# A one-layer hybrid encoder kernel: the last query turns regrouped, four output-weight loads and splits moved to later slots

## The chip, the cores and the metric

The kernel runs on one core of a Trainium2 chip. The metric is the device time of one execution in microseconds (us), and the median over runs is what counts. Three runs of the kernel before gave 1401.51, 1400.05 and 1415.82 us. One further execution was recorded by the hardware profiler, and all views quoted here come from it. Its engines are called PE (TensorE, matrix products; PEld is its load of weights into the array), DVE (VectorE), ACT (ScalarE), POOL (GpSimd) and SP (SyncE, which here only issues transfers). "SPq", "ACTq" and "POOLq" are the queues of those engines.

## The reference: what is computed

The input is a sequence `x` of 2048 tokens with 1024 channels, laid out as a grid of 32 rows and 64 columns. One layer is applied:

```python
shift, scale, gate = split(silu(c) @ w_ada + b_ada, 3)
h = rmsnorm(x, norm_w) * (1 + scale) + shift
na_q, na_k, na_v, na_z, ml_q, ml_k, ml_v, ml_o, ml_z, gates = split(h @ w_in + b_in)
na_out = neighbourhood_attention(na_q, na_k, na_v, rpb) * silu(na_z)   # 8 heads of 64, window 8 x 16 on the grid
ml_out = norm(mlstm_forward + mlstm_backward, sigmoid(ml_o)) * silu(ml_z)   # 4 heads of 128
y = concatenate([na_out, ml_out]) @ w_out
return rmsnorm(x + gate * y, final_norm_w)
```

All of it is float32. The change touches how `na_q` (the attention queries, 512 of the columns of `h @ w_in`) is computed at the very end of the input projection, and when the rows of `w_out` are brought in.

## The kernel before, in words

A float32 product is made of three TensorE products of rounded parts (type fp32r). Each operand is split into a high part and a low part: `whi` and `wlo` for weights, `hhi` and `hlo` for activations. The splitting costs one ACT instruction (the high part, a copy) and one subtraction on POOL or DVE (the low part) per block.

**Token groups and weight columns.** The 2048 tokens form four groups of 512, numbered 0 to 3; group g holds the grid rows 8g to 8g+7. The weight columns of the last part of the input projection form 16 slices `s` of 128 columns: `s` 0 to 3 are the mLSTM gate path, 4 to 7 the attention gate path, 8 to 11 the attention keys, 12 to 15 the attention queries. One slice for one group is 24 matrix products of 128 x 512 (8 blocks of the 1024 input channels, three products for each), here called one group-turn. There are 64 of them, 1536 products.

**Turns.** `nq_gen` (L840 to L911) is a Python generator that emits these products one at a time. Its list `turns` says in which order the slices come and which groups each takes; for instance `(12, (1, 0))` is slice 12 for group 1 and then for group 0. Here turn i is the i-th entry of that list. A turn works on weights that lie in one half of a two-place buffer (`whi_a`, `wlo_a`; the half is i modulo 2). A turn needs a new load of weights unless the turn two places before it had the same slice. One load is: a transfer of 512 KB into the single buffer `rawq` (`nq_load`, L826), then the split (`nq_split`: ACT L834 or, for queries, L837; then POOL L835 or, for queries, DVE L838). Both are emitted in the first group of the turn before, after its seventh product, where the split of turn i+1 is followed at once by the load for the turn after it. Since `rawq` has one buffer, a load can start only when the split before it has read the buffer.

**Eviction and stores.** After 24 products ACT (L898) writes the high part of the query result to one of two buffers, which alternate, DVE (L899) writes the low part, and two transfers on ACT's queue store them to a scratch tensor `d_qna` in device memory (L864, 256 KB each, emitted after the seventh product of the next group-turn; L911 for the last). The eviction two group-turns later writes the same buffer again and so has to wait until these stores are done.

**The way into phase 2.** `pump(n)` takes n products from the generator; earlier stages (the mLSTM passes, `ml_pass2`) use it to fill PE. Phase 2 then does the attention in 16 patches of 8 x 16 queries with four units (pairs of heads) each: 64 units. `slot(n)` issues, in an order written out by hand, the scores of unit n (`stage_s`: PE L1336/L1337, DVE L1342, ACT L1343), the product with the values of unit n-2 (`stage_o`: PE L1379, DVE L1381), the transposes of unit n-1 (`stage_t`: PE L1364, ACT L1366), loads, the normalisation of unit n (`stage_n`, DVE), whatever the table `first` has for this slot, and at last `pump(22)` (12 from slot 5 on). Slots begin when 108 or fewer of the 1536 products are left; slot 4 pumps all that remain. From slot 5 on the pump takes products of the output projection (`outproj`, L1416): first weights 4 to 7 for both halves of the 1024 output columns, 12 products for each half, then weights 0 to 3.

**Output weights.** `w_out` has 8 blocks of 512 KB, already multiplied by the gate and kept in device memory as `d_wo`. They have no space of their own: blocks 0 to 3 are loaded over the low part of group 0's activations and split into the place of its high part; blocks 4 to 7 take the place of group 1. `load_w` (L1311) uses POOL's queue for blocks 0 to 3 and SP's for 4 to 7. Blocks 0 to 3 are loaded by the last turn itself (`lastload`), as its products leave the space; blocks 4 to 7 by the table `first`. `split_w` (L1316: ACT L1317, then DVE L1318) makes high and low parts. Before it can use blocks 4 to 7, group 1 must have had its last query turn.

**Order on an engine.** Each engine executes its instructions in the order given; a wait holds all that comes behind it on that engine or queue. Inside the slots the order is the one written out; before them a planner places instructions by priority. ACT, for example, has in slot 5: the conversion of the mLSTM half of the first patch (`mix_high`, L1389, first use of the output projection), the exponentials of unit 5, the conversion of the attention half (L1389 again), the copies of unit 4's transposes, and the rest.

Of the kernel before, what the change touches and what calls it, by code (L numbers as in the profile page):

```python
# [15 lines left out]
P = 128  # L16
# [38 lines left out]
def patch_ps(ap):  # L55
    return ap.rearrange("p (a r k) -> p a r k", a=4, k=16)


class Kernel:
# [762 lines left out]
    def nq_load(self, i, s):  # L822

        nc = self.nc
        raw = self.raw.tile([P, 4, 256], F32, tag="raw0", name=f"rawq_{i}").rearrange("p a b -> p (a b)").rearrange("p (k c) -> p k c", k=KT)
        (nc.gpsimd if i >= 27 else nc.sync).dma_start(raw, self.w_main[10 + s // 2, :, :, (s % 2) * P : (s % 2 + 1) * P])  # L826
        return i, s, raw

    def nq_split(self, i, s, raw):
# [10 lines left out]
    def nq_gen(self):  # L840
        nc = self.nc
        whi, wlo = self.wslot[0]
        both, upper, lower = range(NG), (3, 2), (1, 0)
        turns = [(s, both) for s in (0, 1, 2, 3)] + [(s, upper) for s in (4, 5, 6, 7, 8, 9, 10, 11, 12, 14, 13, 15)]
        turns += [(s, lower) for s in (8, 9, 10, 11, 4, 5, 6, 7)]
        turns += [(15, (1,)), (13, (1,)), (14, (1,)), (12, (1, 0)), (14, (0,)), (13, (0,)), (15, (0,))]
        order = [(i, s, g) for i, (s, gs) in enumerate(turns) for g in gs]
        needs = [i for i, (s, gs) in enumerate(turns) if i == 1 or i > 1 and s != turns[i - 2][0]]
        raw = self.nq_load(needs[0], turns[needs[0]][0])
        late, parity = [], False  # L850
        for i, s, g in order:
            off = (i % 2) * P
            kind, ct = ("mz", "nz", "k", "q")[s // 4], s % 4
            patch = kind != "k"
            col = {"mz": 20, "nz": 8, "k": 4, "q": 0}[kind] + ct
            bias = self.bcol[:, col : col + 1]
            ps = self.pp.tile([P, GT], F32, tag="pp", name=f"pq_{s}_{g}")
            for k in range(KT):
                w1, w2 = whi[:, k, off : off + P], wlo[:, k, off : off + P]
                for n, (w, h) in enumerate(((w1, self.hhi), (w1, self.hlo), (w2, self.hhi))):  # L860
                    nc.tensor.matmul(patch_ps(ps) if patch else ps, w, self.htok(h, g, k, patch), start=(k == 0 and n == 0), stop=(k == KT - 1 and n == 2))  # L861
                    if k == 2 and n == 0:
                        while late:
                            nc.scalar.dma_start(*late.pop(0))  # L864
                    if i == len(turns) - 1 and k % 2 and n == 2:
                        self.lastload(k // 2)
                    if k == 2 and n == 0:
                        if needs and needs[0] == i + 1:
                            needs.pop(0)
                            self.nq_split(*raw)  # L870
                            if needs:
                                raw = self.nq_load(needs[0], turns[needs[0]][0])
                    if k < KT - 1 or n < 2:
                        yield
            if kind == "k" and g in lower:

                for j in range(2):
                    rows, other = slice(j * HD, (j + 1) * HD), slice((1 - j) * HD, (2 - j) * HD)
                    cols = slice(j * T + g * GT, j * T + (g + 1) * GT)
                    hv = self.kk[ct][rows, cols]  # L880
                    nc.scalar.activation(hv, ps[rows], AF.Identity, bias=bias[rows])
                    nc.vector.scalar_tensor_tensor(self.kk[ct][other, cols], ps[rows], bias[rows], hv.bitcast(F32), ALU.add, ALU.subtract)
                yield
                continue
            parity = not parity
            if parity:
                both = self.qst.tile([P, 1032], F32R, tag="st", name=f"qst_{s}_{g}")
            else:
                both = self.raw.tile([P, 1024], F32R, tag="raw1", name=f"qst_{s}_{g}")
            hv, lv = both[:, 0:512], both[:, 512:1024]  # L890
            if kind in ("mz", "nz"):
                hv = hv.bitcast(F32)
                nc.scalar.activation(hv, ps, AF.Silu, bias=bias)
                dst = (self.d_zna if kind == "nz" else self.d_zml)[4 * g : 4 * g + 4, :, ct].rearrange("a p q -> p a q")
                nc.scalar.dma_start(dst, hv.rearrange("p (a q) -> p a q", a=4))
                self.zdone.add((kind, ct, g))
            else:
                nc.scalar.activation(hv, ps, AF.Identity, bias=bias)  # L898
                nc.vector.scalar_tensor_tensor(lv, ps, bias, hv.bitcast(F32), ALU.add, ALU.subtract)  # L899
                for e, part in enumerate((hv, lv)):  # L900
                    src = part.bitcast(F32).rearrange("p (a q) -> p a q", a=4)
                    if kind == "q":
                        dst = self.d_qna[e, ct // 2, 4 * g : 4 * g + 4, :, ct % 2].rearrange("a p q -> p a q")
                    else:
                        dst = self.d_kna[e, ct * P : (ct + 1) * P, g * GT : (g + 1) * GT].rearrange("p (a q) -> p a q", a=4)
                    late.append((dst, src))
            if (s, g) in ((15, 3), (15, 2)):
                self.freed.append(g)
            yield
        while late:  # L910
            nc.scalar.dma_start(*late.pop(0))  # L911
# [287 lines left out]
    def phase2(self):  # L1199
        nc = self.nc  # L1200
# [13 lines left out]
        b0, last_b = patches[0], patches[-1]  # L1214
# [66 lines left out]
        def load_z(b):  # L1281
            nc.gpsimd.dma_start(zs[pos[b] % 2], self.d_zna[b])
# [5 lines left out]
        def load_m(b):  # L1288
            nc.gpsimd.dma_start(mix_parts(b)[1][:, 4:, :].bitcast(F32), self.d_mix[b])

        def load_x(b):
            pr, pc = divmod(b, 4)
            x = flat(self.raw.tile([P, 4, 256], F32, tag=f"raw{pos[b] % 2}", name=f"xr_{b}"))
            nc.gpsimd.dma_start(x, xg[8 * pr : 8 * pr + 8, 16 * pc : 16 * pc + 16, :])
            L[b]["x"] = x
# [15 lines left out]
        def load_w(k):  # L1311
            (nc.gpsimd if k < 4 else nc.sync).dma_start(wolo[k].bitcast(F32), self.d_wo[k])
# [3 lines left out]
        def split_w(k):  # L1316
            nc.scalar.activation(wohi[k], wolo[k].bitcast(F32), AF.Copy)  # L1317
            nc.vector.tensor_tensor(wolo[k], wolo[k].bitcast(F32), wohi[k].bitcast(F32), ALU.subtract)  # L1318
# [148 lines left out]
        for t in pbuf:  # L1467
            nc.vector.memset(t, 0.0)
        b1 = patches[1]

        first = {
            0: [lambda: nc.sync.dma_start(zs[1], self.d_mix[b0])],
            1: [lambda: load_w(4), lambda: load_w(5)],
            2: [lambda: load_w(6), lambda: load_w(7)],
            3: [lambda: split_w(4), lambda: split_w(5)],
            4: [lambda: split_w(6), lambda: split_w(7), lambda: load_x(b0)],
            5: [lambda: load_z(b1)],
            6: [lambda: load_m(b1), lambda: split_w(0), lambda: split_w(1), lambda: load_x(b1)],
            7: [lambda: split_w(2), lambda: split_w(3)],
            8: [load_fnw],  # L1480
# [147 lines left out]
```

## Time and profile before

| quantity | value |
|---|---|
| runs | 1401.51, 1400.05, 1415.82 us; median 1401.51 |
| profiled execution | 1398.06 us, its span from first to last instruction 1396.2 us |
| mean granted TensorE clock | 0.987 |
| PE busy | 1310.7 us, 8052 products |
| DVE, ACT, POOL busy | 834.0, 529.7, 294.5 us |
| transfers | 264.72 MB, mean 190 GB/s |

The profiled execution is 3.45 us shorter than the median. Times inside it are counted from its first instruction. In a timeline row the first number is the start, the second the duration, then engine, line, operation, output and inputs; in brackets stands how long the engine had been idle before, and what released it. A row of waits gives the total, the number and the longest in us. A row of windows gives the stretch, its length, busy time and count of each engine, the granted clock (1.00 is full), the busy share of the 16 transfer engines (1 or a little over means that they are all busy) and GB/s. A group row gives the shortest, middle and longest duration in ns.

### The profile page before, as it was taken

Reading aid. Unit: us, or ns where it says so; the run is one execution under the profiler, and the core shown is the slowest. Engines: PE = TensorE matmul, PEld = TensorE weight load, DVE = VectorE, ACT = ScalarE, POOL = GpSimd, SP = SyncE. Lnnn points to the kernel's source line nnn. Section 1 sums busy time; section 2 is a strip of 40 time slices with the busy share of each in tenths; the row PEclk is TensorE's granted clock in tenths of the full one; section 3 lists DMA queues with packets and bytes.
Section 4 is the critical chain, followed back from the end, with each engine's and each line's share of the span. In section 5 each row is a group of like instructions: output and inputs, shape, how many; then the busy total and the mean of one; then the engine's idle time right before and its main releaser. Section 6 shows DMA issues by size and latency. Waiting matters only on the chain. (4 is left out here: it accounts for less than half of the span.)

```text
span 1396.2 us, 23375 instructions
## 1 busy us (share of the span) xinstructions
PE 1310.7 (94%) x8052; PEld 1124.3 (81%) x8052; DVE 834.0 (60%) x2565; ACT 529.7 (38%) x1131; POOL 294.5 (21%) x324
## 2 busy tenths in 40 slices
PE   2989999998999999999999998899998999999996
PEld 2989998898887787888888886788776888888885
DVE  6683423211355669067758876877536777777674
ACT  4642344532222323113323223323345555555551
POOL 4353221433101110002212011112412211111111
PEclk9999999999999999999999999999999999999999
DMA  9798548778367675455766868745779896876862
GB/s 315 230 301 206 122 124 222 203 189 208 109 129 210 141 194 163 144 167 159 212 189 216 251 204 232 211 131 168 203 210 253 184 233 158 196 197 170 192 161 75
DMA packets 269100, 264.72 MB, mean 190 GB/s; under 512 B 33499, under 2 KB 229083, under 8 KB 268983
## 3 DMA queue, kind: packets, MB, share of 16 engines
q1 hardware_dynamic: 177022, 185.92, 49.4%
q0 software_dynamic: 21936, 39.30, 11.5%
q10 hardware_dynamic: 70024, 38.02, 9.6%
q8 instruction: 64, 1.05, 0.3%
q14 instruction: 54, 0.43, 0.1%
HBM read 178.62 MB, written 92.72 MB: 194 GB/s over the span
## 5 line engine op out<-in xcount | busy, mean ns | idle before, releaser
L861 PE MATMUL pq<-hhi,whi_a 128*128 128x512 f32 x512 | 211.6, 413 | 5.6 <-ACT whi_a L837 4.8
L861 PE MATMUL pq<-hhi,wlo_a 128*128 128x512 f32 x512 | 211.7, 414 | 0.5 <-DVE wlo_a L838 0.5
L861 PE MATMUL pq<-hlo,whi_a 128*128 128x512 f32 x512 | 211.4, 413 | 0.0
L861 PEld LDWEIGHTS pq<-hhi,whi_a 128*128 128x128 f32 x512 | 98.4, 192 | 24.6 <-ACT whi_a L837 5.6
L1343 ACT ACTIVATE pbuf<-pbuf,mn 128x480 f32<-128x480 f32 (+5 forms) x128 | 76.3, 597 | 104.4 <-DVE mn L1342 104.4
L861 PEld LDWEIGHTS pq<-hhi,wlo_a 128*128 128x128 f32 x512 | 98.3, 192 | 19.1 <-DVE wlo_a L838 1.0
L861 PEld LDWEIGHTS pq<-hlo,whi_a 128*128 128x128 f32 x512 | 98.1, 192 | 18.1
L1416 PE MATMUL y<-hhi,whi_a 128*128 128x512 f32 x256 | 85.9, 405 | 3.7 <-ACT whi_a L1389 3.7
L1416 PE MATMUL y<-hhi,wlo_a 128*128 128x512 f32 x256 | 84.3, 399 | 0.0
L835 POOL TENSOR_TENSOR wlo_a<-rawq,whi_a 128x1024 fp32r<-128x1024 f32 x20 | 48.0, 2398 | 166.1 <-ACT whi_a L834 91.9
L1111 POOL TENSOR_TENSOR hm<-hm,ck 128x128 f32<-128x128 f32 x64 | 26.3, 412 | 265.2 <-DVE hm L1110 179.9
L425 PE MATMUL pvo<-whi_b,hhi 128*128 128x256 f32 x256 | 74.0, 289 | 6.9 <-DVE stvo L495 6.9
L1342 DVE CUSTOM_DVE_ANT_0 pbuf<-pS,tab 128x480 f32<-128x480 f32 (+5 forms) x128 | 64.8, 540 | 26.0 <-PE pS L1337 18.4
L1019 DVE TENSOR_SCALAR wv<-kv,gtile 128x129 f32<-128x129 f32 x120 | 38.7, 328 | 63.0 <-PE dc L1035 34.8
L1092 ACT ACTIVATE num<-px,gtile 128x129 f32<-128x129 f32 x120 | 38.2, 364 | 98.4 <-PE px L1087 76.9
L426 PE MATMUL pvo<-wlo_b,hhi 128*128 128x256 f32 x256 | 72.8, 284 | 0.0
L427 PE MATMUL pvo<-whi_b,hlo 128*128 128x256 f32 x256 | 72.8, 284 | 0.0
L495 DVE TENSOR_TENSOR stvo<-pvo,brow 128x256 f32<-128x256 f32 x64 | 26.5, 420 | 72.7 <-PE pvo L427 56.6
L710 ACT ACTIVATE dec<-dec,gtile 128x128 f32<-128x128 f32 x128 | 42.0, 392 | 68.9 <-POOL dec L706 52.4
L460 DVE TENSOR_TENSOR stv<-pv,brow 128x256 f32<-128x256 f32 x32 | 12.9, 422 | 84.9 <-PE pv L427 37.5
L1379 PE MATMUL pO<-pt,v 128*64 128x128 f32 (+3 forms) x832 | 60.5, 280 | 0.5 <-ACT pt L1366 0.5
L1364 PE MATMUL pT<-ident,pbuf 128*128 128x128 f32 (+2 forms) x416 | 59.1, 280 | 0.0
(299 smaller groups left out, 3578.8 us busy)
## 6 DMA issues: line engine op xcount, KB each, us to landing
ck<-d_ck SPq DMA_DIRECT2D x64, 384.5 KB
kv<-d_ck SPq DMA_DIRECT2D x120, 128.5 KB
rawq<-in_w_main_dram SPq DMA_DIRECT2D x27, 512.0 KB
raw<-in_w_main_dram SPq DMA_DIRECT2D x20, 512.0 KB
d_ck<-stvo SPq DMA_DIRECT2D x16, 514.0 KB
x<-in_x_dram SPq DMA_DIRECT2D x16, 512.0 KB
wada<-in_w_ada_dram SPq DMA_DIRECT2D x32, 256.0 KB
dec<-d_mneg SPq DMA_DIRECT2D x32, 256.0 KB
```

The lines of the kernel that those rows point to most:

```text
L425: nc.tensor.matmul(ps, lhi(k), rhi(k), start=(k == 0), stop=False)
L426: nc.tensor.matmul(ps, lhi(k), rlo(k), start=False, stop=False)
L427: nc.tensor.matmul(ps, llo(k), rhi(k), start=False, stop=(k == KT - 1))
L710: nc.scalar.activation(t[:, d, o, :], t[:, d, o, :], AF.Exp, bias=self.cols["g"][:, d, h, c : c + 1])
L835: nc.gpsimd.tensor_tensor(lo[:, :, cs], raw, hi[:, :, cs].bitcast(F32), ALU.subtract)
L861: nc.tensor.matmul(patch_ps(ps) if patch else ps, w, self.htok(h, g, k, patch), start=(k == 0 and n == 0), stop=(k == KT - 1 and n == 2))
L1019: nc.vector.tensor_scalar(wv, tiles[d, i][:, 128:257], self.cols["w"][:, d, h, c : c + 1], None, ALU.mult)
L1342: nc.vector.tensor_tensor_reduce(pt[:, :nk], ps, tabs[place[u]][j][:, :nk], 1.0, 3e38, ALU.add, ALU.min, mn)
L1343: nc.scalar.activation(pt[:, :nk], pt[:, :nk], AF.Exp, bias=mn, scale=-1.0, accum_out=sums[:, j : j + 1])
L1364: nc.tensor.transpose(ps[:cs, i, :], pts[j][:, i * cs : (i + 1) * cs], self.ident)
L1379: nc.tensor.matmul(po[j * HD : (j + 1) * HD, :], v[:n, h * HD : (h + 1) * HD], pt[j][:n, i, :], start=(i == 0), stop=(i == nch - 1))
L1416: nc.tensor.matmul(y, m[:, k, :], w[k][:, cs], start=(k == 4 and n == 0), stop=(k == 3 and n == 2))
```

## The change

Three things are edited. The load of a query turn always goes to SP's queue (before, turns from 27 on used POOL's). The tail of the list of turns is rewritten: slices 15 and 14 take groups 1 and 0 in one turn each, slice 13 takes group 1, slice 12 groups 1 and 0, and slice 13 group 0 last, with the weights that still lie in its half of the buffer. There are 29 turns in place of 31, and the same 64 group-turns. And the table `first` loads output weights 4 to 7 in slot 3 (before: 4 and 5 in slot 1, 6 and 7 in slot 2), splits 4 and 5 in slot 4 and 6 and 7 in slot 5 (before: slots 3 and 4).

```diff
-        (nc.gpsimd if i >= 27 else nc.sync).dma_start(raw, self.w_main[10 + s // 2, :, :, (s % 2) * P : (s % 2 + 1) * P])
+        nc.sync.dma_start(raw, self.w_main[10 + s // 2, :, :, (s % 2) * P : (s % 2 + 1) * P])
...
         turns += [(s, lower) for s in (8, 9, 10, 11, 4, 5, 6, 7)]
-        turns += [(15, (1,)), (13, (1,)), (14, (1,)), (12, (1, 0)), (14, (0,)), (13, (0,)), (15, (0,))]
+        turns += [(15, (1, 0)), (14, (1, 0)), (13, (1,)), (12, (1, 0)), (13, (0,))]
...
             0: [lambda: nc.sync.dma_start(zs[1], self.d_mix[b0])],
-            1: [lambda: load_w(4), lambda: load_w(5)],
-            2: [lambda: load_w(6), lambda: load_w(7)],
-            3: [lambda: split_w(4), lambda: split_w(5)],
-            4: [lambda: split_w(6), lambda: split_w(7), lambda: load_x(b0)],
-            5: [lambda: load_z(b1)],
+            3: [lambda: load_w(4), lambda: load_w(5), lambda: load_w(6), lambda: load_w(7)],
+            4: [lambda: split_w(4), lambda: split_w(5), lambda: load_x(b0)],
+            5: [lambda: split_w(6), lambda: split_w(7), lambda: load_z(b1)],
             6: [lambda: load_m(b1), lambda: split_w(0), lambda: split_w(1), lambda: load_x(b1)],
             7: [lambda: split_w(2), lambda: split_w(3)],
```

Turns are numbered from 0; the old tail is turns 24 to 30, the new one 24 to 28.

## The prediction

> **What bounds the kernel now.** I read the page first, then the waits of PE from the region of the change to the end, and then the timelines of that region, engine by engine.
>
> ```profile
> PE 1310.7 (94%) x8052; PEld 1124.3 (81%) x8052; DVE 834.0 (60%) x2565; ACT 529.7 (38%) x1131; POOL 294.5 (21%) x324
> PE pq L861 <- ACT whi_a L837: 4.8, 2, 2.6
> PE y L1416 <- ACT whi_a L1389: 3.7, 1, 3.7
> PE pq L861 <- DVE wlo_a L838: 0.5, 1, 0.5
> PE pO L1379 <- ACT pt L1366: 0.5, 1, 0.5
> 1066.00:1396.00 330.00, 317.75 (x2158) 259.14 (x2156) 234.48 (x784) 166.07 (x449) 58.50 (x93) 0.99 0.72 174
> ```
>
> PE is busy 94% of the span. The four rows behind it are all of PE's waits from 1000 us to the end: 9.5 us. Two turns wait for the split of their weights (L837, L838), and the first output projection waits for ACT (L1389). From 1066 us on PE is busy 317.75 of 330 us and waits 0.5, so what PE gains or loses ahead of 1066 arrives at the end one for one.
>
> ```profile
> 1003.47 0.40 PE L861 MATMUL pq<-hhi,wlo_a 128*128 128x512 f32 x1
> 1006.11 0.50 PE L861 MATMUL pq<-hhi,whi_a 128*128 128x512 f32 x1 [2.24 <-ACT whi_a L837]
> 1014.03 0.29 PE L1336 MATMUL pS<-hhi,qhigh 128*128 128x288 f32 x1
> 1016.90 0.52 PE L861 MATMUL pq<-hhi,whi_a 128*128 128x512 f32 x1 [2.58 <-ACT whi_a L837]
> 1020.81 0.40 PE L861 MATMUL pq<-hhi,wlo_a 128*128 128x512 f32 x1
> 1036.03 0.40 PE L861 MATMUL pq<-hlo,whi_a 128*128 128x512 f32 x1
> 1040.78 0.40 PE L861 MATMUL pq<-hhi,whi_a 128*128 128x512 f32 x1
> 1006.10:1010.60 4.50, 3.98 (x10) 2.90 (x11) 1.87 (x2) 0.53 (x1) 2.99 (x5) 0.62 1.07 254
> 1016.90:1020.80 3.90, 3.90 (x11) 3.24 (x12) 2.62 (x6) 2.12 (x3) 0.91 (x1) 0.56 0.51 130
> ```
>
> Between 1036.03 and 1040.78 lie 20 steps of undisturbed products: 0.2375 us from start to start, 5.70 for a group-turn. Turn 25 ends with the product at 1003.47. Turn 26's 24 products should fill 1003.71 to 1009.41, but the next instruction starts at 1014.03: 4.62 us lost. From there to 1020.81 PE does 11 products (the row's x11: three for scores, eight of turn 27) and the score product at 1014.03: 8 times 0.2375 plus 4 times 0.13 (288 columns in place of 512) is 2.42 of 6.78 us, so 4.36 lost. Together 8.98 us, though the waits name only 5.3 of it: the rest is the clock, 0.62 and 0.56 behind the two gaps.
>
> The Trainium skill, page "TensorE: Matmul & The Clock Gate", section "Why this matters for your kernels", asks for no idle gaps above some 3 us. By it gaps of 2.24 and 2.58 us would leave the clock alone and the term would be 5.3 us; the two window rows disagree, and I keep 8.98.
>
> **Why the turns wait.**
>
> ```profile
> L826 SPq DMA_DIRECT2D rawq<-in_w_main_dram x27: 539/547/842, 506.2 to 997.8; - x27
> 1005.00 1.06 ACT L837 ACTIVATE whi_a<-rawq 128x1024 fp32r<-128x1024 f32 x1 [5.06 <-DMA rawq<-in_w_main_dram]
> 1006.09 1.23 DVE L838 SCALAR_TENSOR_TENSOR wlo_a<-rawq,whi_a 128x1024 fp32r<-128x1024 f32 x1 [4.12 <-ACT whi_a L837]
> 1007.61 0.93 POOL L826 DMA_DIRECT2D rawq<-in_w_main_dram  x1 [3.09 <-DMA d_qna<-qst]
> 1015.79 1.06 ACT L837 ACTIVATE whi_a<-rawq 128x1024 fp32r<-128x1024 f32 x1 [9.16 <-DMA rawq<-in_w_main_dram]
> 1019.21 0.96 SPq L1309 DMA_DIRECT2D tab<-d_t  x2
> ```
>
> One buffer makes a chain: transfer (997.8 to 1005.00: 7.2 us on SP; 1007.61 to 1015.79: 8.2 on POOL), ACT 1.06, DVE 1.23. That is 9.5 to 10.5 us per new slice, while turns 25 and 26 have 5.7 us of products each.
>
> **The change part by part.** I keep the clock of this trace. *New turns.* Turn 24 (slice 15, two groups) fills what turns 24 and 25 fill now, up to 1003.71; turn 25 (slice 14) then fills 1003.71 to 1015.1. Its split is done before 997.8, as turn 25's is now: the load at 997.8 needs the buffer that it reads. The load of turn 26 starts at 997.8 as now; its split comes at turn 25's seventh product, 1005.4, when the transfer has landed (1005.00), and ends at 1007.7. The load of turn 27 starts on SP then and lands by 1014.9 to 1015.9. Turn 26 starts near 1015.6 (0.5 for unit 0's scores), reaches its split at 1017.3, has both parts at 1019.6, and turn 27 needs them at 1021.3: no wait, 1.7 us of room. Turn 28 has its weights. Removed: 8.98 us. The load of turn 27 moves from POOL past SP's queue; nothing waits behind it there, since SP's next issue is the unit-0 table at 1019.21.
>
> *Two loads and splits less* (turns 29 and 30): two transfers of 512 KB, 2 x 1.06 us of ACT, 2 x 1.23 of DVE. In the trace they lie under running products, so PE gains nothing directly; but POOL's `xr` load no longer sits behind the last of them, and moves some 6 us ahead, out of the crowded stretch.
>
> ```profile
> 1044.83 0.60 POOL L1294 DMA_DIRECT2D xr<-in_x_dram  x1 [6.23 <-DVE wlo_a L838]
> 1040.28 1.36 ACTq L864 DMA_DIRECT2D d_qna<-qst  x2
> 1053.23 2.00 ACT L1317 ACTIVATE hhi<-hlo 128x1024 fp32r<-128x1024 f32 x2
> 1058.61 0.69 ACT L898 ACTIVATE qst<-pq,bcol 128x512 fp32r<-128x512 f32 x1 [3.37 <-DMA qlow<-d_qna]
> 1060.52 0.63 ACT L1389 ACTIVATE whi_a<-gtile 128x512 fp32r<-128x512 f32 x1 [1.23 <-DVE qst L899]
> 1064.05 0.84 ACT L1366 ACTIVATE pt<-pT 120x384 f32<-120x384 f32 x2
> 1054.32 2.36 DVE L1318 TENSOR_TENSOR hlo<-hlo,hhi 128x1024 fp32r<-128x1024 f32 x2 [0.32 <-ACT hhi L1317]
> 1054.87 0.40 PE L861 MATMUL pq<-hhi,wlo_a 128*128 128x512 f32 x1
> 1061.20 0.50 PE L1416 MATMUL y<-hhi,whi_a 128*128 128x512 f32 x1 [3.68 <-ACT whi_a L1389]
> 1065.77 0.32 PE L1336 MATMUL pS<-hhi,qhigh 128*128 128x360 f32 x1
> 1061.20:1065.80 4.60, 4.60 (x13) 3.38 (x14) 3.27 (x10) 2.53 (x7) 1.53 (x3) 0.63 1.06 308
> ```
>
> *The third stall.* The last product ends at 1055.3, but its eviction L898 starts only at 1058.61: its buffer still holds what the stores issued at 1040.28 carry, 18 us under way. (The row names another transfer landing at about that time; only a store frees this buffer.) Behind the eviction in ACT's order stands L1389, for which PE waits. The loads of output weights 6 and 7 went out just ahead of those stores:
>
> ```profile
> 1039.20 1.05 SPq L1312 DMA_DIRECT2D hlo<-d_wo  x2
> 1041.02 0.29 PE L1336 MATMUL pS<-hlo,qhigh 128*128 128x288 f32 x1
> 1044.94 7.17 SPq L1309 DMA_DIRECT2D tab<-d_t  x4
> 1040.00:1070.00 30.00, 26.32 (x155) 20.83 (x155) 17.79 (x44) 16.57 (x36) 5.73 (x10) 0.94 1.06 289
> q1 hardware_dynamic: 767, 1.54, 55.3%
> tab<-d_t SPq DMA_DIRECT2D x2, 180.0 KB
> q1 hardware_dynamic: 640, 0.71, 22.0%
> ```
>
> From 1040 to 1070 the transfer engines are full (1.06). With the change no output weights go out ahead of these stores (slot 3 begins at 1041.02), so I take the eviction at 1055.3 and L1389, 1.91 behind it, at 1057.2.
>
> *Splits 6 and 7 in slot 5.* They now stand behind the transpose copies, whose end lies 4.37 us behind L1389's start (1064.89 less 1060.52): 1061.6. ACT takes 1.0 each: 1062.6 and 1063.6; DVE 1.18 each, up to 1065.1. The twelve products of slot 5 begin at 1058 with weights 4 and 5, stop after six near 1059.4, and end two products behind the last low part, 1065.6 to 1066.0 at either clock. Unit 6's scores start at 1065.77 now. So the third stall changes its cause and keeps its size: 0 to 0.3 us. The slow clock behind it, which the last row above gives as 0.63 up to 1065.8, ends over a microsecond later and reaches into slot 6: about 0.5, an estimate.
>
> *Loads 4 to 7 in slot 3.* SP issues them behind the two tables of slot 3, which wait for DVE's use of unit 3's scores (1041.02): by 1043 if DVE, freed of turn 30's split, is prompt, by 1046 if as now. Splits 4 and 5 take 2 us of ACT ahead of the eviction at 1055.3, so they cost nothing if both blocks are there by 1053.3. Tables and two blocks are 1.42 MB; q1, which carries SP's issues, moved 1.54 MB in 10 us from 1040 and 0.71 in 12 us from 1050 (the two q1 rows; MB stand second, 180 KB is one table). At the first rate they are there 9.2 us later, 1052.2 to 1055.2: 0 to 1.9 us late. At the second, 24 us later. I take the first, since then the queue had work throughout; cost 0.5.
>
> The sum is -9.0 + 0.3 + 0.5 + 0.5 = -7.7 us. The profiled execution, 1398.06 (span 1396.2 and 1.9 around it), becomes 1390.4. The median of the runs stands 3.45 higher, at 1401.51, and becomes **1393.8**.
>
> **The rivals.**
>
> *The transfers take the gain back.* Output weights 4 and 5 (1.05 MB) move into a stretch already full: at its 289 GB/s that is 3.6 us more. Against it: `xr` and one load of weights leave its beginning. If PE has to wait for all of it: 1397.4. The Trainium skill, page "DMA: Bandwidth & Descriptors", section "Issuing engines are not separate DMA queues", says that transfers issued by any engine run on the same 16 engines and interleave; by it what is bunched on SP's queue delays POOL's and ACT's transfers as well, which is this rival. No row shows yet whether PE would wait for it.
>
> *The chain still stalls.* Turn 26 still has one group, with a new slice behind it. If the load of turn 27 lands after 1019, turn 27 waits, at a loss like 4.36 now: 1398.2. For it: a room of 1.7 us only, and stores now come every 5.7 us.
>
> *The third stall goes too.* If ACT's work in slot 5 is placed so that nothing waits, the twelve products take 2.85 us from 1057.5 (1061.20 less 3.68) and unit 6 begins at 1060.4, 5.4 us sooner: with -9.0 it is 1387.1. Against it: the splits stand behind the copies.
>
> *Slower than before.* The four loads crawl on SP's queue, and split 4, in ACT's order ahead of the last eviction and of L1389, holds both, and PE with them. At the lower rate the two blocks land 24 us after 1043 to 1046, 1067 to 1070, 14 to 17 us late; less 9.0 the kernel loses 5 to 8 us: 1406 to 1409. It decides from about 9 us of lateness, landing beyond 1062. Against it: the low rate was measured when SP itself was often waiting, with little queued.
>
> **How the numbers follow.** Forecast 0.56 (1391.5 to 1396), transfers 0.16, chain 0.08, third stall gone 0.12, slower 0.08. The range 1388 to 1399 leaves out the slower case and the ends of the others. Two per cent, 28 us, is about what a measurement of this kernel can tell from no change. All of PE's waits and slow clock near the change are below 15 us, and the slower case would have to be four times as late: faster 0.02, same 0.96, slower 0.02.
>
> **What would show it.** Right: no wait of PE for L837 or L838 after 1000 us and a granted clock of 1.00 up to slot 5; 28 loads on SP and none on POOL; the last eviction starting as its products end; PE's one wait in slot 5 naming L1317 or L1318. Wrong: a wait of L1317 for `d_wo`, which would hold the eviction; L837 waiting for `rawq` in turn 26; the eviction still waiting for a transfer; or new waits of PE beyond slot 6.

## The result and the profile after

The changed kernel takes 1398.8 us (median of 22 runs, 1393.48 to 1405.39); the kernel before, run beside it, 1407.26 (median of 22, 1398.8 to 1415.82). The ratio is 0.994, 95% interval 0.9921 to 0.9958. The forecast was a gain of 7.7 us; the medians differ by 8.5. The forecast time of 1393.8 was 5.0 too low, because it was built on a median before of 1401.51 from three runs; that 1398.8 lies inside the range of 1388 to 1399, by 0.2 us, is luck.

The profiled execution of the changed kernel took 1396.22 us, span 1394.1: only 2.1 less than the one before. The two executions differ ahead of the change. A mark that both have is the first of the last four transposes of the mLSTM stage (PE, L1144), some 5 us before the first wait that the change removes. The timeline of PE before:

```profile
998.94 0.27 PE L1144 MATMUL ht<-perm,hm 128*128 128x128 f32 x1
```

and after, with the products that matter behind it:

```profile
1004.00 0.28 PE L1144 MATMUL ht<-perm,hm 128*128 128x128 f32 x1
...
1050.90 0.40 PE L861 MATMUL pq<-hhi,wlo_a 128*128 128x512 f32 x1
...
1054.13 0.50 PE L1416 MATMUL y<-hhi,whi_a 128*128 128x512 f32 x1 [0.58 <-ACT whi_a L1389]
...
1058.82 0.79 PE L1416 MATMUL y<-hhi,whi_a 128*128 128x512 f32 x1 [2.77 <-ACT hhi L1317]
...
1060.08 0.80 PE L1416 MATMUL y<-hlo,whi_a 128*128 128x512 f32 x1 [0.47 <-DVE hlo L1318]
...
1062.38 0.50 PE L1336 MATMUL pS<-hhi,qhigh 128*128 128x360 f32 x1
...
1068.33 0.32 PE L1336 MATMUL pS<-hlo,qhigh 128*128 128x360 f32 x1
```

The execution after reached the mark 5.06 us later, over stages whose code is the same. So all comparisons below count from this mark; from it on each of the two has 162 products of the projection to do. From it to the last product of the input projection: 55.93 us before (998.94 to 1054.87), 46.90 after. To the first score product of slot 6: 66.83 and 58.38. To that of slot 7: 71.61 (the row at 1070.55) and 64.33, 7.28 less. To the end of the span: 397.26 and 390.1, 7.16 less. The traced execution before (1398.06) is shorter than all 22 timed ones (1398.8 and up), so a difference of traces against it makes a kernel look somewhat worse than the medians do.

```profile
1070.55 0.33 PE L1336 MATMUL pS<-hlo,qhigh 128*128 128x360 f32 x1
```

The waits of PE after, from the mark to the end, and windows from the mark to the last product, over slot 5, and over slot 6 (the granted clock stands third from the end):

```profile
PE y L1416 <- ACT hhi L1317: 2.8, 1, 2.8
PE y L1416 <- ACT whi_a L1389: 0.6, 1, 0.6
PE y L1416 <- DVE hlo L1318: 0.5, 1, 0.5
PE pO L1379 <- ACT pt L1366: 0.3, 1, 0.3
```
```profile
1004.00:1051.30 47.30, 47.30 (x249) 38.25 (x248) 20.79 (x55) 19.05 (x42) 10.61 (x18) 1.00 0.95 279
1051.30:1062.38 11.08, 7.26 (x34) 4.65 (x34) 6.40 (x13) 5.75 (x11) 3.54 (x6) 0.81 1.07 303
1062.38:1068.33 5.95, 5.95 (x34) 4.86 (x33) 3.34 (x10) 3.89 (x8) 0.00 (x0) 0.79 0.52 124
```

The waits for L837 and L838 are gone, and PE is busy 47.30 of 47.30 us at full clock. All 28 loads into the single buffer are on SP:

```profile
L826 SPq DMA_DIRECT2D rawq<-in_w_main_dram x28: 539/547/632, 512.7 to 1012.3; - x28
```

In slot 5 PE now waits for the splits of output weights 6 and 7 (L1317, L1318), and the slow clock reaches into slot 6. ACT, and the issues of SP, over the same stretch:

```profile
1022.30 0.69 ACT L898 ACTIVATE qst<-pq,bcol 128x512 fp32r<-128x512 f32 x1 [2.64 <-DMA d_qna<-qst]
1024.36 1.06 ACT L837 ACTIVATE whi_a<-rawq 128x1024 fp32r<-128x1024 f32 x1 [1.37 <-DMA rawq<-in_w_main_dram]
1047.39 2.00 ACT L1317 ACTIVATE hhi<-hlo 128x1024 fp32r<-128x1024 f32 x2
1051.33 0.69 ACT L898 ACTIVATE qst<-pq,bcol 128x512 fp32r<-128x512 f32 x1 [1.95 <-PE pq L861]
1053.45 0.63 ACT L1389 ACTIVATE whi_a<-gtile 128x512 fp32r<-128x512 f32 x1 [1.43 <-DVE qst L899]
1057.72 1.99 ACT L1317 ACTIVATE hhi<-hlo 128x1024 fp32r<-128x1024 f32 x2
```
```profile
1037.04 0.30 PE L1336 MATMUL pS<-hlo,qhigh 128*128 128x288 f32 x1
1038.90 1.80 SPq L1312 DMA_DIRECT2D hlo<-d_wo  x4
```

The last eviction starts as its products end (1051.33), splits 4 and 5 wait for nothing, and the four loads go out 1.9 us after slot 3's first score product.

### The profile page after: what moved, and what is told of

It is laid out like the page before. It is cut to its first block, busy times and chain, and to the rows that moved or that the text cites. A ratio compares the mean times of both kernels' runs of the same rounds, so it can differ in the third digit from the quotient of the medians.

```text
span 1394.1 us, 23365 instructions
## 1 busy us (share of the span) xinstructions
PE 1312.1 (94%) x8052; PEld 1124.8 (81%) x8052; DVE 828.9 (59%) x2563; ACT 527.9 (38%) x1129; POOL 294.3 (21%) x321
## 4 chain that ended last, share of the span: by engine, by line
PE 53%; DMA 6%; DVE 3%; issue 2%; ACT 1%; POOL 1%; POOLq 0%; SPq 0%; ACTq 0%; DVEq 0%
PE pq L861 21%; PE y L1416 11%; PE pO L1379 4%; PE pT L1364 4%; DMA kv<-d_ck 2%; PE pi L1089 2%; PE pc L425 2%; PE pc L426 2%; PE pc L427 2%; PE px L1087 2%; PE pS L1336 1%; PE pS L1337 1%; PE dc L1035 1%; DMA tab<-d_t 1%; PE a L1074 1%
## 5 line engine op out<-in xcount | busy, mean ns | idle before, releaser
L710 ACT ACTIVATE dec<-dec,gtile 128x128 f32<-128x128 f32 x128 | 42.0, 392 | 71.6 <-POOL dec L706 60.8
L1379 PE MATMUL pO<-pt,v 128*64 128x128 f32 (+3 forms) x832 | 61.3, 282 | 0.3 <-ACT pt L1366 0.3
```

Of the source, the lines that this page charges most:

```text
L710: nc.scalar.activation(t[:, d, o, :], t[:, d, o, :], AF.Exp, bias=self.cols["g"][:, d, h, c : c + 1])
L1379: nc.tensor.matmul(po[j * HD : (j + 1) * HD, :], v[:n, h * HD : (h + 1) * HD], pt[j][:n, i, :], start=(i == 0), stop=(i == nch - 1))
```

## The experiments

In all runs the measure is the time from the same transposes to the last product of the projection and to slot 7 (55.9 and 71.6 before, 46.9 and 64.3 after), and the ratio to the kernel before. The ratio comes from several runs; each stretch is that of one traced execution.

**Only the new turns.** The kernel before with the new tail of `turns` and the loads on SP; the table `first` unchanged:

```diff
-        (nc.gpsimd if i >= 27 else nc.sync).dma_start(raw, self.w_main[10 + s // 2, :, :, (s % 2) * P : (s % 2 + 1) * P])
+        nc.sync.dma_start(raw, self.w_main[10 + s // 2, :, :, (s % 2) * P : (s % 2 + 1) * P])
...
-        turns += [(15, (1,)), (13, (1,)), (14, (1,)), (12, (1, 0)), (14, (0,)), (13, (0,)), (15, (0,))]
+        turns += [(15, (1, 0)), (14, (1, 0)), (13, (1,)), (12, (1, 0)), (13, (0,))]
```

> Only the new turns and the queue of their loads; the table of slots as before. The stretch from the first of the last four transposes L1144 to the first score product of slot 7 took 71.6 us before (998.94 to 1070.55) and 64.3 after. Theory (the gain is the chain of one buffer under turns of one group): both waits for L837 go, 9.0 us less, whatever the table does. The loads of output weights 4 and 5, now asked for while group 1 is in use, hold SP's queue from slot 1 to the end of group 1's turn and then go out just ahead of the query stores, so the last eviction is late again and the third stall stays near 3.7 us of wait: stretch 62 to 64, ratio about 0.994. Rival (the held SP queue costs more than the turns bring: tables and query loads late): new waits of PE in slots 2 to 4, stretch over 66.

Measured: ratio 1.0031 (1.0003 to 1.0059), 67.0 us to the last product and 78.0 to slot 7. The longest waits of PE:

```profile
PE pq L861 <- DMA hlo<-d_wo: 15.9, 2, 9.9
```

Neither account holds as written. No wait for L837 or L838 is left, as the first says, but the time went elsewhere, and SP was not held. The program now emits the loads of output weights ahead of group 1's last turn, which reads the same place; so the order of dependence turns round, and PE waits for the loads, 15.9 us. In this run slice 12 of group 1 was computed with output weights where the low parts of its activations had been. The new turns can't stand without a later place for these loads: the first half of the edit forces the second.

**Only the new table.** The kernel before with loads 4 to 7 in slot 3, splits in slots 4 and 5.

```diff
-            1: [lambda: load_w(4), lambda: load_w(5)],
-            2: [lambda: load_w(6), lambda: load_w(7)],
-            3: [lambda: split_w(4), lambda: split_w(5)],
-            4: [lambda: split_w(6), lambda: split_w(7), lambda: load_x(b0)],
-            5: [lambda: load_z(b1)],
+            3: [lambda: load_w(4), lambda: load_w(5), lambda: load_w(6), lambda: load_w(7)],
+            4: [lambda: split_w(4), lambda: split_w(5), lambda: load_x(b0)],
+            5: [lambda: split_w(6), lambda: split_w(7), lambda: load_z(b1)],
```

> Only the new table (output weights 4 to 7 loaded in slot 3, split in slots 4 and 5); the turns as before. Theory: the two waits for L837, 4.8 us with 0.5 for L838, stay with their slow clock; the last eviction is no longer late, and PE waits in slot 5 for L1317 (about 2.8 us) in place of L1389 (3.7): stretch 71 to 74 us, ratio 0.999 to 1.002. Rival (the gain comes from moving the loads out of the way of other transfers): the waits for L837 shrink and the stretch is 64 to 67, ratio near 0.995.

Measured: ratio 1.0043 (1.0022 to 1.0064); 57.0 us to the last product, 84.8 to slot 7. (To the end the trace is 13.6 us longer than the one before, the median 5.3.) The first waits of PE, then ACT's part of slots 4 and 5:

```profile
PE y L1416 <- ACT whi_a L1389: 10.7, 1, 10.7
PE pq L861 <- ACT whi_a L837: 6.3, 2, 4.6
```
```profile
1055.44 1.06 ACT L1317 ACTIVATE hhi<-hlo 128x1024 fp32r<-128x1024 f32 x1 [3.44 <-DMA hlo<-d_wo]
1057.85 1.06 ACT L1317 ACTIVATE hhi<-hlo 128x1024 fp32r<-128x1024 f32 x1 [1.35 <-DMA hlo<-d_wo]
...
1058.99 0.69 ACT L898 ACTIVATE qst<-pq,bcol 128x512 fp32r<-128x512 f32 x1
1064.88 3.13 ACTq L911 DMA_DIRECT2D d_qna<-qst  x2
1068.07 0.63 ACT L1389 ACTIVATE whi_a<-gtile 128x512 fp32r<-128x512 f32 x1 [8.39 <-DMA tab<-d_t]
```

The waits of the turns stay, so the gain is not the table's. But the table alone is worse than I allowed: the splits wait 3.4 and 1.4 us for their loads, ACT holds the eviction behind them, and then the last stores start only 5 us after it. This is the first half of the prediction's slower case, in a kernel in which turn 30's load and split are still there (the loads go out at 1046.04, 4.5 us after slot 3's start at 1041.55, not 1.9).

```profile
1041.55 0.30 PE L1336 MATMUL pS<-hlo,qhigh 128*128 128x288 f32 x1
1046.04 2.85 SPq L1312 DMA_DIRECT2D hlo<-d_wo  x4
```

**The chain of one buffer.** The kernel before, old turns, old table; the transfers of turns 26 and 27 left out.

```diff
+        if i in (26, 27):
+            return i, s, self.lastraw
         raw = self.raw.tile([P, 4, 256], F32, tag="raw0", name=f"rawq_{i}")...
...
+        self.lastraw = raw
```

> The kernel before, with the two transfers of weights for turns 26 and 27 left out: their splits take turn 25's weights again, so slice 14 of group 1 and slice 12 of groups 1 and 0 are computed from the wrong weights, by the same number of instructions. All turns keep their order and their one group. Theory (the waits for L837 are the transfer through one buffer): both waits and the slow clock behind them go; from the first of the last four transposes to the last product of the projection 55.9 us become 47 to 48 (46.9 in the changed kernel), and the stretch to slot 7 71.6 becomes 62 to 64, ratio 0.993 to 0.995. Rival (turns of one group wait in any case, for ACT and DVE or for the query stores): waits of several us stay, 51 us or more to the last product.

Measured: 46.97 us to the last product, as in the changed kernel to 0.1 us, and no wait for L837 or L838; ratio 0.9938 (0.9913 to 0.9962). So the transfer through one buffer is what turns of one group waited for, clock included. To slot 7 it took 65.3, over the 64 that I had allowed. The last eviction and PE's one wait (lines 901 and 1392 here are 898 and 1389 elsewhere):

```profile
1050.85 0.69 ACT L901 ACTIVATE qst<-pq,bcol 128x512 fp32r<-128x512 f32 x1 [5.53 <-DMA d_qna<-qst]
PE y L1419 <- ACT whi_a L1392: 6.0, 1, 6.0
```

The eviction waits 5.5 us for the store, where it waited 3.4 before, and PE 6.0 where it waited 3.7. The products came sooner; the store that frees the buffer was issued at 1030.17, behind loads 6 and 7, and the eviction came 20.7 us later.

**Loads 6 and 7 elsewhere.** The kernel before with these two in slot 1.

```diff
-            1: [lambda: load_w(4), lambda: load_w(5)],
-            2: [lambda: load_w(6), lambda: load_w(7)],
+            1: [lambda: load_w(4), lambda: load_w(5), lambda: load_w(6), lambda: load_w(7)],
```

> The kernel before, with output weights 6 and 7 loaded in slot 1, behind 4 and 5, and not in slot 2. In the old order of turns group 1 is done by then. Theory (the last eviction is late because 1 MB of these loads goes out just ahead of the stores that free its buffer): the eviction starts within 0.3 us of the end of the last product, PE's wait for L1389 falls from 3.7 to under 1 us, and with the slow clock behind it the stretch falls from 71.6 to 66 to 68 us, ratio 0.996 to 0.998. The two waits for L837 stay. Rival (the stores are late because all transfers share full engines, wherever these two are issued): eviction late by 2 us or more, stretch 70 to 73.

Measured: ratio 0.9984 (0.9965 to 1.0004), 71.8 us to slot 7, PE's wait for L1389 3.1. ACT:

```profile
1047.63 1.06 ACT L837 ACTIVATE whi_a<-rawq 128x1024 fp32r<-128x1024 f32 x1 [4.54 <-DMA d_qna<-qst]
1060.55 0.67 ACT L898 ACTIVATE qst<-pq,bcol 128x512 fp32r<-128x512 f32 x1
```

The last eviction no longer waits for a transfer. But it starts 2 us late all the same: ACT was held 4.5 us ahead of turn 30's split, and its work piled up. (The row names a store, but the transfer of turn 30's weights, issued at 1039.11, landed 8.5 us later, just then; before, it took 5.9.) So the run doesn't show whether the store that frees the buffer, issued at 1043.12, would have been there at the end of the products, 1058.5. My price was wrong in any case: moving these two loads alone brought no gain that is clear of zero.

**All four splits in slot 4.** The changed kernel with one line moved.

```diff
-            4: [lambda: split_w(4), lambda: split_w(5), lambda: load_x(b0)],
-            5: [lambda: split_w(6), lambda: split_w(7), lambda: load_z(b1)],
+            4: [lambda: split_w(4), lambda: split_w(5), lambda: split_w(6), lambda: split_w(7), lambda: load_x(b0)],
+            5: [lambda: load_z(b1)],
```

> The changed kernel with the splits of output weights 6 and 7 in slot 4, behind those of 4 and 5. Theory (PE's wait in slot 5 is these splits standing behind the copies of the transposes): the waits for L1317 and L1318, 2.8 and 0.5 us, go, and the slow clock behind them, 6.8 us at half speed, goes with them; what stays is the 0.6 us for L1389: stretch 64.3 less 5 to 6.6, 58 to 59 us, ratio 0.989 to 0.991. Rival (blocks 6 and 7 are not there yet in slot 4, and ACT, waiting for them, holds the last eviction and L1389): ACT waits for the transfer at L1317, PE for L1389, stretch 63 to 67.

Measured: 58.8 us to slot 7, ratio 0.9888 (0.986 to 0.9916). PE's waits to the end, and slot 5:

```profile
PE y L1416 <- ACT whi_a L1389: 1.3, 1, 1.3
PE pO L1379 <- ACT pt L1366: 0.8, 1, 0.8
PE y L1416 <- DVE hlo L1318: 0.2, 1, 0.2
```
```profile
1049.30:1056.04 6.74, 5.41 (x36) 3.91 (x35) 4.92 (x12) 3.31 (x8) 2.44 (x4) 1.00 1.05 343
```

The blocks are there in slot 4, the wait and the slow clock go. The wait in slot 5 was the place of two splits in ACT's order.

**Loads inside the turn.** The changed kernel with loads 4 to 7 emitted by the last turn of group 1 as its products leave the space, and splits in slots 3 and 4.

```diff
+                    if i == len(turns) - 2 and g == 1 and k % 2 and n == 2:
+                        self.lastload(4 + k // 2)
...
-            3: [lambda: load_w(4), lambda: load_w(5), lambda: load_w(6), lambda: load_w(7)],
-            4: [lambda: split_w(4), lambda: split_w(5), lambda: load_x(b0)],
-            5: [lambda: split_w(6), lambda: split_w(7), lambda: load_z(b1)],
+            3: [lambda: split_w(4), lambda: split_w(5)],
+            4: [lambda: split_w(6), lambda: split_w(7), lambda: load_x(b0)],
+            5: [lambda: load_z(b1)],
```

> The changed kernel, with output weights 4 to 7 loaded inside the last turn of group 1, each block when the products that read its place are done (as blocks 0 to 3 are in the last turn), and split in slots 3 and 4 as before. Theory: loads go out some 3 to 8 us earlier, nothing of slots 3 to 5 waits for a split: stretch 57.5 to 59 us, ratio 0.989 to 0.991, as in the run with the splits in slot 4. Rival (2 MB ahead of the query stores on the full transfer engines make these late, as before): the last eviction starts late by 1 to 4 us, PE waits for L1389 by as much: stretch 60 to 64.

Measured: 61.3 us to slot 7, ratio 0.9915 (0.9888 to 0.9943). The rival came nearer: the last eviction started 0.7 us late and PE waited 1.8.

```profile
1034.15 0.69 ACT L900 ACTIVATE qst<-pq,bcol 128x512 fp32r<-128x512 f32 x1 [1.72 <-PE pq L861]
1039.42 0.93 ACTq L864 DMA_DIRECT2D d_qna<-qst  x2
```

ACT issued the stores 4.6 us after the eviction that they follow, just as SP's load issues ended (1036.47 to 1039.51). Whether these loads hold the issue was not settled.

```profile
1036.47 3.04 SPq L1314 DMA_DIRECT2D hlo<-d_wo  x3
```

**Turn 27's load on POOL.** Meant was the changed kernel with the old line for the queue.

> The changed kernel with the load of turn 27 back on POOL's queue. Theory (turn 27 has some 1.7 us of room, and a load on POOL took 1 us longer than one on SP): no wait of PE for L837 or under 0.5 us, stretch 64 to 65.5 us as in the changed kernel (64.3), ratio 0.993 to 0.996. Rival (the room is used up): PE waits for L837 or L838 in turn 27 for 1 us or more, with a slow clock behind it, stretch 66 to 68.

The kernel that ran is the changed kernel line for line, without this edit; its trace has all 28 loads on SP:

```profile
L826 SPq DMA_DIRECT2D rawq<-in_w_main_dram x28: 540/546/632, 507.7 to 1009.6; - x28
```

So it says nothing of the queue, which stays untested. It is a second measurement of the changed kernel, in another series: 46.9 us to the last product, 64.0 to slot 7, ratio 0.9933 (0.9905 to 0.996), no wait for L837, and the same three waits in slot 5 (0.4, 2.8 and 0.5).

**Conversion ahead of the last eviction.** The run with all splits in slot 4, and L1389 emitted before the last L898 and its stores (the generator stops once more after its last product; slot 5 converts and then lets it finish).

```diff
                 mix_high(b0, 1)
                 mix_low(b0, 1)
+                self.pump(2)
+                self.owed = 0
...
-                    if k < KT - 1 or n < 2:
+                    if k < KT - 1 or n < 2 or i == len(turns) - 1:
...
-                self.pump(max(0, self.left) + 1)
+                self.pump(max(0, self.left))
```

> As the run with all four splits in slot 4, and the last eviction with its stores emitted behind the first conversion for the output projection (L1389) and not ahead of it. Theory (PE's wait of 1.3 us there is ACT's eviction and its two issues of stores, the second waiting for DVE): L1389 starts as the products end, PE waits for it 0.7 us or less, stretch 58.8 becomes 57.5 to 58.4, ratio 0.987 to 0.989. Rival (the later eviction is missed elsewhere: its buffer or its stores are waited for in slots 6 to 8): stretch 59 or more, new waits of PE behind slot 5.

Measured: no wait for L1389, 58.5 us to slot 7, ratio 0.9913 (0.9891 to 0.9935): nothing gained. A wait in slot 7 came in its place:

```profile
1059.40 0.29 DVE L1381 TENSOR_TENSOR gtile<-pO,gtile 128x128 f32<-128x128 f32 x1 [5.71 <-DMA gtile<-d_zna]
```

DVE waits 5.7 us for the gate values of the second patch, and PE 2.4 behind it. Slot 10 began at 78.4 us, where the run with the splits in slot 4 had 76.0. (A wait of 0.5 us for L838 in turn 27 lies ahead of all that this edit touches. Counted from the last product, slot 7 came after 10.6 us for 11.9, and slot 10 after 30.5 for 29.1.)

**Fewer transfers.** The run with the early conversion, without the transfers of output weights 1 to 3.

```diff
-                    if i == len(turns) - 1 and k % 2 and n == 2:
-                        self.lastload(k // 2)
+                    if i == len(turns) - 1 and k == 1 and n == 2:
+                        self.lastload(0)
```

> As the run with the conversion ahead of the last eviction, with the transfers of output weights 1, 2 and 3 left out (1.5 MB): their splits take what lies in their place, so the output projection uses wrong weights for these blocks, by the same instructions. In that run DVE waited 5.7 us in slot 6 for the gate values of the second patch (L1381 for d_zna) and PE 2.4 us behind it, and slot 10 began 78.4 us after the transposes. Theory (these values are late because the output weights are ahead of them on full transfer engines): DVE's wait falls under 1 us, PE's goes, slot 10 begins at 73 to 75.5. Rival (they are late because they can be asked for only when the first half of the mix is converted, whatever else moves): DVE's wait stays over 3 us.

Measured: DVE's wait 1.0 us, PE's gone, slot 10 at 74.9; ratio 0.9903 (0.9874 to 0.9933). The gate values were late because of the 1.5 MB ahead of them.

**Gate values first.** Output weights 2 and 3 loaded in slot 5 behind those values: on the run with the splits in slot 4, and on the one with the early conversion.

```diff
-                    if i == len(turns) - 1 and k % 2 and n == 2:
+                    if i == len(turns) - 1 and k in (1, 3) and n == 2:
                         self.lastload(k // 2)
...
-            5: [lambda: load_z(b1)],
+            5: [lambda: load_z(b1), lambda: load_w(2), lambda: load_w(3)],
```

> As the run with all four splits in slot 4, and output weights 2 and 3 loaded in slot 5 behind the gate values of the second patch, not in the last turn ahead of them; they are split in slot 7 as before. There DVE waited 3.1 us for these values and slot 10 began 76.0 us after the transposes. Theory (crowded transfers): DVE waits 0 to 1.5 us, slot 10 begins at 74 to 75.5, ratio 0.986 to 0.989. Rival (the two blocks are now late for slot 7): ACT waits at L1317 for d_wo there, PE behind it, slot 10 at 76 or later.

> The same move of output weights 2 and 3, on the run with the conversion ahead of the last eviction (slot 10 at 78.4, DVE's wait 5.7, PE's 2.4). Theory: DVE waits under 2 us, PE not at all behind slot 5, slot 10 begins at 73.5 to 75, the soonest of all, ratio 0.985 to 0.989. Rival (late blocks 2 and 3, or query stores in the way): PE waits of over 1 us in slots 6 to 9, slot 10 at 76 or later.

Measured: the first 0.9887 (0.9855 to 0.9919), slot 10 at 75.5, no wait of DVE for the values; the second 0.9891 (0.986 to 0.9921), slot 10 at 77.3, where I expected 75 at most. In the second, DVE waits 1.3 us, and time is lost in turn 27 and in slots 6 to 9:

```profile
PE pO L1379 <- ACT pt L1366: 2.3, 3, 1.0
PE pq L861 <- ACT whi_a L837: 1.3, 1, 1.3
PE pq L861 <- DVE wlo_a L838: 0.5, 1, 0.5
```

The wait in turn 27 is not the doing of this edit, since the code up to there is that of the run with the splits in slot 4, which had 0.7 us of room. Counted from the last product, slot 10 came after 29.1 us with the splits in slot 4, 30.5 with the early conversion, 26.7 with fewer transfers, and 27.1 and 28.0 here. So the later loads of blocks 2 and 3 bring some 2 us up to slot 10, in one execution each; the ratios don't show it. The four versions with the splits in slot 4 and all transfers (0.9887 to 0.9913) can't be told apart by their intervals; the simplest of them, one moved line, already beats the kernel before, and its interval (0.986 to 0.9916) lies below that of the changed kernel (0.9921 to 0.9958), though the two were taken in different series.

## Why the prediction was right, point by point

- *The two waits of the turns, -8.98 us.* Right in cause and size. Measured 9.03 (55.93 to 46.90), and 8.96 where only the transfers were left out. The share of the clock, 3.7 us, was in it.
- *Turn 27 without a wait, 1.7 us of room.* Right that it doesn't wait; the room was too large. After, the low part is done at 1026.67 and needed by the turn's third product at 1028.04: 1.4 us. Six more traces have the same code up to turn 27: room of 1.5, 0.7 and 0.5 us, and waits of 0.5, 0.8 and 1.8. So the room differs from one execution to the next by more than its size. I had left out of it that the eviction ahead of the split in ACT's order waits for a store (2.64 us at 1022.30 above; 6.31 in the execution with the wait of 1.8). That stores follow each other closely was the reason I had given for the rival of the chain.

```profile
1025.45 1.22 DVE L838 SCALAR_TENSOR_TENSOR wlo_a<-rawq,whi_a 128x1024 fp32r<-128x1024 f32 x1 [1.68 <-ACT whi_a L837]
1028.04 0.40 PE L861 MATMUL pq<-hhi,wlo_a 128*128 128x512 f32 x1
```

- *The load of turn 27 past SP's queue, 0.* Right that nothing waits behind it on SP: it was issued at 1012.3, SP's next transfer at 1018.55. What POOL would have cost in the new order was not tried.
- *The patch's `xr` load some 6 us ahead.* Larger: 1044.83 before, 45.9 us behind the mark; after it was at 1026.97, 23.0 behind, and so 13.9 us sooner beyond the 9.0 that all moved.

```profile
1026.97 0.60 POOL L1294 DMA_DIRECT2D xr<-in_x_dram  x1 [10.18 <-DMA d_qna<-qst]
```

- *The last eviction on time, L1389 1.91 us behind it.* Right: 2.12 (1051.33 to 1053.45). That loads 6 and 7 had held its store fits, but is not shown. With them just ahead of the stores (before, and with the turns' transfers left out) the eviction came 18.3 and 20.7 us behind the issue of its store, and waited 3.4 and 5.5 us. With them in slot 3 (after) it came 15.0 us behind and did not wait; with them in slot 1 it came 17.4 us behind, held by other work. But in the run with the loads inside the turn three such loads went out just ahead of the stores, and the eviction, 11.2 us behind, did not wait.
- *Splits 6 and 7 in slot 5, +0.3.* Right that the third stall changes its cause and keeps its size. From the last product to slot 6 it took 10.90 us before (1054.87 to 1065.77) and 11.48 after: +0.58.
- *A slow clock in slot 6, +0.5.* Mis-sized: slot 6 took 5.95 us where it had taken 4.78, +1.17. PE had gaps of 0.58, 2.77 and 0.47 us in slot 5, and the clock rows are 0.81 and then 0.79.
- *Loads 4 to 7 in slot 3, +0.5.* Mis-sized: 0. DVE, freed of turn 30's split, was prompt, the loads went out 1.9 us into slot 3, and the splits waited for nothing. The run with the table alone shows the other end that I had named: out after 4.5 us, 3.4 and 1.4 us of waiting, and more behind it.
- *The sum, -7.7.* Measured -7.28 to slot 7, -7.16 to the end in the profile, -8.5 between the medians. That the two mis-sized terms nearly cancel (+0.7 and -0.5) is luck.
- *The rivals.* The transfers do not take this gain back, but they take the next one, as the traces of the runs with the gate values show. The slower case needed loads out late; it came true for a kernel with half of the change. The chain's rival came true by up to 1.8 us of wait, in executions whose code is the changed kernel's up to turn 27.
- *The time itself, 1393.8.* The base was mis-sized, not the step: three runs gave 1401.51 where 22 gave 1407.26. The two per cent that I had called the least that can be told from no change was too coarse: 22 runs of each kernel gave an interval of 0.4 per cent.

Of the Trainium skill: the page "TensorE: Matmul & The Clock Gate" asks for no idle gaps above some 3 us (section "Why this matters for your kernels"). The runs disagree once more: a gap of 1.81 us in the run with the loads inside the turn was followed by a clock of 0.64 (first row). But the length of the gap alone doesn't decide: one of 1.33 in the run with the splits in slot 4 left the clock at 1.00, and so did one of 1.78, with 0.51 behind it, in the run with the table alone (second row). What else decides was not tried.

```profile
1053.90:1058.60 4.70, 4.68 (x12) 3.41 (x13) 3.29 (x10) 2.54 (x7) 1.63 (x3) 0.64 1.09 372
1005.00:1011.00 6.00, 5.42 (x22) 4.04 (x23) 1.89 (x2) 0.59 (x2) 3.30 (x5) 1.00 1.07 271
```

## What to carry to other kernels

Where a resource with one buffer is refilled once per step, price the step by the whole chain (here transfer, split and split, 10 us) and give it work at least as long; a regrouping that changes no arithmetic took 9.0 us off the stretch up to the last product here. When steps are reordered, follow what the old order guaranteed to everything that reuses its space: half of this edit made PE wait 15.9 us for data that it should not have read. And look at which work stands in front of the wait on the engine that PE waits for: moving two splits one slot ahead in ACT's order took another 5.5 us off the way to slot 7, where the whole change had taken 7.3.

## What the runs showed of the hardware that I had not expected

- The slow clock can cost most of the wait again: before, waits of 5.3 us went with 9.0 us lost (clock 0.62 and 0.56 behind them); after, behind a wait of 2.77 us in slot 5, the clock of slot 6 was 0.79 and the slot 1.17 us longer.
- A store on ACT's queue can be issued long after its data are made: in the run with the table alone the last stores came 5.2 us behind the end of their eviction (1059.68 to 1064.88; the low part was done at 1060.83), in the run with the loads inside the turn 4.6 us. In the second, SP was putting out three loads of 512 KB until then; in the first, its four such loads lay 16 us back. What holds the issue was not tried.
- The same code ahead of the change took 5.06 us more in one profiled execution than in the other, 60% of the whole effect; without a common mark the profile would have shown a gain of 2.1. Seven executions of the same code up to turn 27 came out there with anything from 1.5 us of room to 1.8 us of wait.
